# The next group's state update in front of the chunk's output work, in each step of a chunked scan

## The chip, the cores and the metric

One Trainium2 chip, one of its cores. The metric is device time in microseconds of one execution of the whole program, median of the runs of a kernel. The core has a matrix engine (TensorE: PE for matmuls, PEld for its weight loads), VectorE (DVE), ScalarE (ACT), GpSimd (POOL) and SyncE (SP), which here issues all the DMAs. Each engine works through its own instructions strictly in the order in which they stand in the program, and waits at an instruction until what that one needs is there.

## The reference, cut to what matters

The program is one layer of a network over 1024 latent tokens and 256 context tokens of width 1024. The part that the change touches is a bidirectional state-space scan: 8 groups of 4 heads, chunks of 128 tokens (8 latent chunks and 2 context chunks), and for each direction

```
states   = einsum('bcsgn,bcsgj,bcsgjp->bcgjpn', bc, decay_to_end, xdt)     # per chunk
carry    = carry * chunk_decay + states                                     # from chunk to chunk
cb       = einsum('bclgn,bcsgn->bcgls', cc, bc)
y_diag   = einsum('bcgjls,bcsgjp->bclgjp', cb * lmat, xdt)                  # inside a chunk
y_off    = einsum('bclgn,bcgjpn,bclgj->bclgjp', cc, entering, exp(a_cum))   # from the carried state
```

The carry runs over the chunks forwards in one direction and backwards in the other, so the output of a group's first chunk needs the last state of the backward direction: all states of a group have to stand before its outputs begin. After the scan come a gate, a grouped norm, a Fourier branch, projections, and a gated feed-forward block.

## The kernel before

The stage of the scan walks over 64 ticks, 8 groups of 8 chunks (the loop at L1016). While the outputs of group g are worked out, the states of group g+1 are built, one per tick and two in a group's last tick (9 per group: context and latent chunks). So that PE is never without work, large matmuls of other parts, the projections by which the later stages are fed, are laid between: `run_fill`, whose matmuls are called `fill` in all rows (L203, L204, L205 and L210).

The kernel is written in a layer that records every operation and then orders each engine's instructions by itself, with a timing model of its own; the order in which the operations are written sets who goes first where several could go. The pieces of a tick, by function:

- `state_a(i)` (L869): the chunk's inputs times the decay weights, the forward half on DVE (tile `xwf`, L873), the backward half on POOL (`xwb`, L874). Both tiles have two buffers.
- `state_b(i)` (L877): two matmuls into the PSUM tile `st` (L881, L882), which has one buffer, and then eight DVE operations of 64 columns (L891) that make the new states, `S0` forwards and `S1` backwards, from the state before and `st`. For a group's first state two ACT copies (L887) stand in their place. The next `st` matmul waits until these have read `st`.
- `y_load(c)` (L896): the DMAs of the next chunk, `abc` among them (L900: a row of 1024 numbers spread over the 128 partitions; two buffers).
- `y_a(c)` (L904): matmuls `cb` (L908) and `yo` (L910, L911; L911 reads the backward states `S1`), one PSUM buffer each; eight ACT operations on `abc` (L915), a masked copy on DVE (L917), an exponential on ACT (L918); on DVE the product `G` (L920), `cd` and `dg` (L924, L925) and `y2` (L929); on POOL `xd` (L932, then two additions, L934 and L935).
- `y_b`, `y_b2` (L938, L946), one tick later: the matmuls `yd` (L943, one PSUM buffer) from `G`, then on DVE `yz` (L951, which frees `yd` and needs `xd` complete; then L952), a norm and a scale.
- `y_c` (L963), four ticks later: transposes (`ytr`, L968) and the store.

The weights of the fill matmuls are split into a high part on ACT (`whi`, L198) and a low part on POOL (`wlo`, L199, 128x1024).

The instructions that the change moves belong to the loop at L1016, in the lines L1027 to L1034.

Of the kernel before, what the change touches and what calls it, by code (L numbers as in the profile page):

```python
# [20 lines left out]
NT = L // P  # L21
# [114 lines left out]
def build(nc, tc, h, o, hook=None, stop=None):  # L136
    es = ExitStack()
    with es:
        _build(nc, tc, h, o, hook, stop, es)


def _build(nc, tc, h, o, hook, stop, es):
# [853 lines left out]
    def run_fill(n):  # L996
        while nfill[0] < n:
            nfill[0] += 1
            try:
                next(fill)  # L1000
            except StopIteration:
                return

    groups = {0: Group(0)}
# [9 lines left out]
    nticks = NG * NT  # L1014
    groups[0].y_load(0)
    for n in range(nticks + LAG + 1):  # L1016
        g, c = divmod(n, NT)
        if n < nticks:
            if c == 0 and g + 1 < NG:
                groups[g + 1] = Group(g + 1)  # L1020
                groups[g + 1].load_states()
                groups[g + 1].state_a(0)
        if n >= 1 and n - 1 < nticks:
            groups[(n - 1) // NT].y_b((n - 1) % NT)
            groups[(n - 1) // NT].y_b2((n - 1) % NT)
        if n < nticks:
            groups[g].y_a(c)  # L1027
            if n + 1 < nticks:
                groups[(n + 1) // NT].y_load((n + 1) % NT)
            if g + 1 < NG:  # L1030
                for i in ((c,) if c < 7 else (7, 8)):
                    if i + 1 < 9:
                        groups[g + 1].state_a(i + 1)
                    groups[g + 1].state_b(i)  # L1034
        if n >= LAG and n - LAG < nticks:
            groups[(n - LAG) // NT].y_c((n - LAG) % NT)
        if n < nticks - NT:
            run_fill(8 + FOFF + ((NPRE - 8 - FOFF) * (n + 1)) // (nticks - NT))
        else:
            run_fill(NPRE + int(RT * (n - 55)))  # L1040
# [668 lines left out]
```

## Time and profile before

| | |
|---|---|
| median of 3 runs | 2228.85 us (2227.23 to 2230.65) |
| profiled execution, its own time | 2232.41 us |
| its span in the trace | 2230.6 us |
| PE busy | 2157.4 us, 97% of the span |
| DVE, ACT, POOL busy | 73%, 45%, 31% |
| stage of the scan | from about 612 us (first fill matmul) to about 1155 us |

The span is what lies between the first and the last instruction in the trace; the time of the same execution is 1.8 us longer. Idle time of an engine that is not the bottleneck costs nothing, so the figure to read in this stage is the idle time of PE, and what ended it.

### The profile page before, as it was taken

The numbers are of one execution on the slowest core, as the hardware profiler recorded it, in microseconds if no ns is written. First come the engines' busy times: TensorE is split into PE (matmuls) and PEld (weight loads), VectorE is DVE, ScalarE is ACT, GpSimd is POOL, SyncE is SP. The second block draws the span as 40 slices with busy tenths as digits, with TensorE's granted clock in tenths as the row PEclk, the third lists the DMA queues.
The fourth block names the chain that finished last, engine by engine and source line by source line (L and its number), as shares of the span: only waits on it lengthen the run. The fifth ranks groups of instructions, "written<-read, shape, count | busy, mean of one in ns | idle before, by whom it ended". The sixth has DMA issues, their size and how long they took to land.

```text
span 2230.6 us, 32729 instructions
## 1 busy us (share of the span) xinstructions
PE 2157.4 (97%) x11560; PEld 1805.8 (81%) x11560; DVE 1628.0 (73%) x2795; ACT 996.0 (45%) x2093; POOL 701.7 (31%) x581
## 2 busy tenths in 40 slices
PE   6999999999999999999999999999899999999997
PEld 1778888887798999999889887877687888878876
DVE  5888888998758777877726657946987667774577
ACT  4444444445436667666743222224532333234443
POOL 1532111010125555555521221111243333332222
PEclk9999999999999999999999999999999999999999
DMA  8212223342454555555454556752476244457765
GB/s 285 77 62 95 76 89 129 126 131 99 149 172 151 175 159 173 175 167 175 151 174 177 178 172 226 246 174 81 155 267 238 86 141 145 144 201 232 235 206 179
DMA packets 167388, 360.80 MB, mean 162 GB/s; under 512 B 17580, under 2 KB 57260, under 8 KB 166584
## 3 DMA queue, kind: packets, MB, share of 16 engines
q1 hardware_dynamic: 167224, 358.71, 47.9%
q8 instruction: 91, 1.49, 0.3%
q14 instruction: 73, 0.60, 0.1%
HBM read 267.86 MB, written 90.78 MB: 161 GB/s over the span
## 4 chain that ended last, share of the span: by engine, by line
PE 74%; DVE 10%; DMA 7%; ACT 4%; issue 3%; POOL 1%; SPq 0%; DVEq 0%; POOLq 0%; ACTq 0%
PE mm L496 16%; PE dm L210 8%; PE fp L204 6%; PE fp L205 6%; PE fp L203 5%; DMA abc<-s_a 3%; PE mm L498 3%; PE spq L210 2%; PE fq L204 2%; PE fq L205 2%; ACT abc L915 2%; PE fq L203 2%; PE fill L210 2%; PE fill L203 2%; PE fill L204 2%
## 5 line engine op out<-in xcount | busy, mean ns | idle before, releaser
L199 POOL TENSOR_TENSOR wlo<-wraw,whi 128x1024 fp32r<-128x1024 f32 x80 | 198.2, 2481 | 581.3 <-ACT whi L198 515.2
L198 ACT CAST whi<-wraw 128x1024 fp32r<-128x1024 f32 x123 | 127.8, 1044 | 218.0 <-PE dm L210 79.3
L203 PE MATMUL fill<-whi,hhi 128*128 128x256 f32 x768 | 222.3, 290 | 0.6 <-ACT whi L198 0.4
L433 DVE SCALAR_TENSOR_TENSOR cv<-pad,vecs,cv 128x1282 f32<-128x1282 f32 (+1 forms) x128 | 211.1, 1679 | 9.4 <-ACT cv L430 8.8
L204 PE MATMUL fill<-wlo,hhi 128*128 128x256 f32 x768 | 216.0, 281 | 0.2 <-POOL wlo L199 0.2
L205 PE MATMUL fill<-whi,hlo 128*128 128x256 f32 x768 | 216.0, 282 | 0.0
L915 ACT ACTIVATE abc<-abc,a_all 128x128 f32<-128x128 f32 x512 | 157.7, 389 | 90.7 <-DMA abc<-s_a 86.7
L205 PE MATMUL fp<-m,opl 128*128 128x512 f32 x452 | 179.7, 398 | 4.3 <-DVE opl L1389 4.1
L203 PE MATMUL fp<-m,oph 128*128 128x512 f32 x452 | 179.7, 398 | 2.1 <-ACT m L1432 0.9
L204 PE MATMUL fp<-m,oph 128*128 128x512 f32 x452 | 179.8, 398 | 1.8 <-DVE m L1433 1.7
L496 PE MATMUL mm<-tq,whi 128*128 128x512 f32 x480 | 155.9, 405 | 2.3 <-ACT whi L198 2.3
L203 PEld LDWEIGHTS fill<-whi,hhi 128*128 128x128 f32 x768 | 144.1, 188 | 3.0 <-ACT whi L198 0.5
L204 PEld LDWEIGHTS fill<-wlo,hhi 128*128 128x128 f32 x768 | 144.6, 188 | 1.4 <-POOL wlo L199 0.6
L205 PEld LDWEIGHTS fill<-whi,hlo 128*128 128x128 f32 x768 | 144.3, 188 | 0.5
L496 PE MATMUL mm<-hhi,whi 128*128 128x512 f32 x320 | 127.5, 399 | 3.4 <-DVE pad L572 3.4
L496 PE MATMUL mm<-hlo,whi 128*128 128x512 f32 x320 | 127.6, 399 | 0.0
L496 PE MATMUL mm<-hhi,wlo 128*128 128x512 f32 x320 | 127.3, 399 | 0.0
L917 DVE COPY_PREDICATED abc<-misc,abc 128x512 f32<-128x512 int32 x64 | 52.0, 813 | 83.4 <-ACT abc L915 83.3
L496 PEld LDWEIGHTS mm<-tq,whi 128*128 128x128 f32 x480 | 91.2, 192 | 24.1 <-ACT whi L198 3.3
L205 PEld LDWEIGHTS fp<-m,opl 128*128 128x128 f32 x452 | 85.2, 189 | 26.5 <-DVE opl L1389 5.6
L891 DVE SCALAR_TENSOR_TENSOR S<-S,ead,st 128x64 f32<-128x64 f32 x512 | 104.8, 272 | 0.0
L203 PEld LDWEIGHTS fp<-m,oph 128*128 128x128 f32 x452 | 85.3, 189 | 24.0 <-ACT m L1432 1.3
(412 smaller groups left out, 5888.7 us busy)
## 6 DMA issues: line engine op xcount, KB each, us to landing
abc<-s_a SPq DMA_DIRECT2D x64, 512.0 KB
fraw<-in_wfi SPq DMA_DIRECT2D x44, 512.0 KB
wraw<-in_wxbc SPq DMA_DIRECT2D x32, 512.0 KB
dx<-in_wada SPq DMA_DIRECT2D x32, 512.0 KB
wraw<-in_wzf SPq DMA_DIRECT2D x24, 512.0 KB
gt<-s_gate SPq DMA_DIRECT2D x24, 512.0 KB
fi<-in_wfo SPq DMA_DIRECT2D x22, 512.0 KB
s_cw<-fo SPq DMA_DIRECT2D x44, 256.0 KB
```

Source lines behind the costliest of these rows:

```text
L198: nc.scalar.copy(out=hi[:, :cols], in_=raw[:, :cols])
L199: (eng or nc.gpsimd).tensor_tensor(out=lo[:, :cols], in0=raw[:, :cols], in1=hi[:, :cols].bitcast(F32), op=ALU.subtract)
L203: nc.tensor.matmul(ps, lhsT=a[0], rhs=b[0], start=start, stop=False)
L204: nc.tensor.matmul(ps, lhsT=a[0], rhs=b[1], start=False, stop=False)
L205: nc.tensor.matmul(ps, lhsT=a[1], rhs=b[0], start=False, stop=stop)
L210: nc.tensor.matmul(ps, lhsT=a[i], rhs=b[j], start=start and (i, j) == (0, 0), stop=stop and (i, j) == (1, 0))
L433: nc.vector.scalar_tensor_tensor(out=v[:, :n], in0=pd[:, t:t + n], scalar=cwh[:, 5 * b + t:5 * b + t + 1], in1=v[:, :n], op0=ALU.mult, op1 ...
L496: nc.tensor.matmul(ps, lhsT=lhs[x], rhs=b[i][y], start=i == 0 and (x, y) == (0, 0), stop=i == 3 and (x, y) == (1, 0))
L498: nc.tensor.matmul(cps, lhsT=lhs[x], rhs=(hc_hi, hc_lo)[y][c0 + i], start=first and i == 0 and (x, y) == (0, 0), stop=last and i == 3 and ...
L891: nc.vector.scalar_tensor_tensor(out=sn[:, hd_], in0=S[-1][:, hd_], scalar=decp[:, i, d, 4 * g + j:4 * g + j + 1], in1=sv_[:, hd_], op0=AL ...
L915: nc.scalar.activation(out=abc[:, d, j, :], in_=abc[:, d, j, :], func=AF.Identity, scale=-1.0, bias=a_all[:, c, hd:hd + 1])
L917: nc.vector.copy_predicated(out=E, mask=tri_b.bitcast(mybir.dt.int32)[:, None, :].to_broadcast([P, HPG, P]), data=abc[:, 1])
```

## The change

In each tick the block that advances the next group's states is written in front of `y_a` and `y_load`, where it stood behind them. No operation is added, removed or altered, and the condition around it is the same.

```diff
         if n < nticks:
-            groups[g].y_a(c)
-            if n + 1 < nticks:
-                groups[(n + 1) // NT].y_load((n + 1) % NT)
             if g + 1 < NG:
                 for i in ((c,) if c < 7 else (7, 8)):
                     if i + 1 < 9:
                         groups[g + 1].state_a(i + 1)
                     groups[g + 1].state_b(i)
+            groups[g].y_a(c)
+            if n + 1 < nticks:
+                groups[(n + 1) // NT].y_load((n + 1) % NT)
         if n >= LAG and n - LAG < nticks:
```

The orders that follow are those that the ordering makes of it. First PE in an ordinary tick of group 1 (rows with - stand before, rows with + now, the others in both; `fill` matmuls stand ahead of the piece and behind it; a number behind a tile's name tells one buffer's use from another):

```order
 L205 MATMUL fill_6540<-whi_6413,hlo7_205 128x256
-L943 MATMUL yd_6568<-xh_5330,G_6470 128x64 x4
-L908 MATMUL cb_6582<-cT_6484,bT_6482 128x128
-L910 MATMUL yo_6584<-S0_5796,cT_6484 128x256
-L911 MATMUL yo_6584<-S1_6146,cT_6484 128x256
-L881 MATMUL st_6615<-xwf_6488,bh_6327 128x256
-L882 MATMUL st_6615<-xwb_6489,bh_6331 128x256
+L881 MATMUL st_6586<-xwf_6455,bh_6327 128x256
+L882 MATMUL st_6586<-xwb_6456,bh_6331 128x256
+L943 MATMUL yd_6568<-xh_5330,G_6487 128x64 x4
+L908 MATMUL cb_6599<-cT_6501,bT_6499 128x128
+L910 MATMUL yo_6601<-S0_5763,cT_6501 128x256
```

The state's two matmuls moved from behind the output matmuls to their front, some 2 us of PE work earlier.

Second DVE where group 4 ends, the tick with two states, before:

```order
L929 TENSOR_TENSOR y2_9884<-yo_9865,ead_212 128x512
L925 SCALAR_TENSOR_TENSOR dg_9881<-dt_all_209,dg_9881,rows_213 128x4
L917 COPY_PREDICATED abc_9894<-misc_171,abc_9894 128x512
L873 TENSOR_TENSOR xwf_10009<-xh_9989,wst_all_211 128x256
L891 SCALAR_TENSOR_TENSOR S0_9903<-S0_9809,ead_212,st_9900 128x64 x4
L891 SCALAR_TENSOR_TENSOR S1_9908<-S1_9814,ead_212,st_9900 128x64 x4
L917 COPY_PREDICATED abc_10054<-misc_171,abc_10054 128x512
L873 TENSOR_TENSOR xwf_10056<-xh_9989,wst_all_211 128x256
L891 SCALAR_TENSOR_TENSOR S0_9916<-S0_9903,ead_212,st_9913 128x64 x4
L891 SCALAR_TENSOR_TENSOR S1_9921<-S1_9908,ead_212,st_9913 128x64 x4
```

And the same states on DVE now:

```order
L929 TENSOR_TENSOR y2_9811<-yo_9792,ead_212 128x512
L925 SCALAR_TENSOR_TENSOR dg_9808<-dt_all_209,dg_9808,rows_213 128x4
L873 TENSOR_TENSOR xwf_10009<-xh_9989,wst_all_211 128x256
L891 SCALAR_TENSOR_TENSOR S0_9870<-S0_9780,ead_212,st_9867 128x64 x4
L891 SCALAR_TENSOR_TENSOR S1_9875<-S1_9785,ead_212,st_9867 128x64 x4
L920 TENSOR_TENSOR G_9908<-abc_9817,cb_9893 128x512
L924 SCALAR_TENSOR_TENSOR cd_9910,dg_9911<-cb_9893,misc_171 128x128
L951 TENSOR_TENSOR yz_9859<-xd_9813,yd_9853 128x256
```

Before, each of the two state updates stood right behind a masked copy (`abc_9894` is that of the next group's first chunk, `abc_10054` that of its second). Now no masked copy stands between `dg` and the first of them, and `G`, `cd` and `yz` stand behind it; the second follows later, behind the masked copy of the next group's first chunk.

Third POOL near the end of group 1, where the low parts of two weight tiles are made, before:

```order
L932 TENSOR_TENSOR xd_6912<-xh_5342,dg_6907 128x256
L934 TENSOR_TENSOR xd_6912<-xd_6912,y2_6910 128x256
L935 TENSOR_TENSOR xd_6912<-xd_6912,y2_6910 128x256
L199 TENSOR_TENSOR wlo_6983<-wraw_6980,whi_6982 128x1024
L199 TENSOR_TENSOR wlo_7643<-wraw_7640,whi_7642 128x1024
```

And now:

```order
L932 TENSOR_TENSOR xd_6929<-xh_5342,dg_6924 128x256
L199 TENSOR_TENSOR wlo_6983<-wraw_6980,whi_6982 128x1024
L934 TENSOR_TENSOR xd_6929<-xd_6929,y2_6927 128x256
L199 TENSOR_TENSOR wlo_7643<-wraw_7640,whi_7642 128x1024
L874 TENSOR_TENSOR xwb_7119<-xh_6325,wst_all_211 128x256
L935 TENSOR_TENSOR xd_6929<-xd_6929,y2_6927 128x256
```

The two weight splits stood behind the chunk's three `xd` operations; now they stand between the first of them and the last, with the state's product `xwb`.

## Rows read from the trace of the kernel before

**Rows 1.** The page's first part: engine, busy us, share of the span, instructions.

```profile
PE 2157.4 (97%) x11560; PEld 1805.8 (81%) x11560; DVE 1628.0 (73%) x2795; ACT 996.0 (45%) x2093; POOL 701.7 (31%) x581
```

**Rows 2.** PE's waits, 625 to 1160 us: line, awaited, us in total, times, longest.

```profile
PE st L881 <- DVE S L891: 6.8, 10, 1.7
PE st L881 <- issue: 3.5, 2, 1.9
PE yo L911 <- DVE S L891: 2.9, 2, 1.5
PE cb L908 <- DVE cd L924: 1.1, 1, 1.1
PE yo L910 <- DVE y L929: 0.8, 1, 0.8
PE st L881 <- ACT S L887: 0.7, 1, 0.7
```

**Rows 3.** PE's timeline: start, us, engine, line, operation, idle before and its releaser.

```profile
683.87 0.67 PE L881 MATMUL st<-xwf,bh 128*128 128x256 f32 x2 [1.71 <-DVE S L891]
...
765.87 0.59 PE L881 MATMUL st<-xwf,bh 128*128 128x256 f32 x2
...
812.08 0.67 PE L881 MATMUL st<-xwf,bh 128*128 128x256 f32 x2 [1.86 <-issue]
...
965.08 0.67 PE L881 MATMUL st<-xwf,bh 128*128 128x256 f32 x2 [1.31 <-DVE S L891]
...
1026.02 0.67 PE L881 MATMUL st<-xwf,bh 128*128 128x256 f32 x2 [1.52 <-DVE S L891]
...
1032.71 0.70 PE L911 MATMUL yo<-S,cT 128*128 128x256 f32 x2 [1.48 <-DVE S L891]
```

**Rows 4.** PE's timeline, for the pace of each kind of matmul.

```profile
660.21 0.28 PE L204 MATMUL fill<-wlo,hhi 128*128 128x256 f32 x1
660.32 0.59 PE L881 MATMUL st<-xwf,bh 128*128 128x256 f32 x2
660.75 0.59 PE L882 MATMUL st<-xwb,bh 128*128 128x256 f32 x2
...
687.61 1.00 PE L943 MATMUL yd<-xh,G 128*128 128x64 f32 x8
688.45 0.44 PE L908 MATMUL cb<-cT,bT 128*128 128x128 f32 x2
688.72 0.60 PE L910 MATMUL yo<-S,cT 128*128 128x256 f32 x2
```

**Rows 5.** DVE's timeline in a tick with two weight splits on POOL.

```profile
804.44 2.13 DVE L952 TENSOR_TENSOR yz<-yz,zs 128x256 f32<-128x256 f32 x1
...
810.36 1.61 DVE L891 SCALAR_TENSOR_TENSOR S<-S,ead,st 128x64 f32<-128x64 f32 x8
```

**Rows 6.** POOL's timeline in the same tick: a weight split, an addition.

```profile
803.89 2.39 POOL L199 TENSOR_TENSOR wlo<-wraw,whi 128x1024 fp32r<-128x1024 f32 x1
...
811.67 0.73 POOL L935 TENSOR_TENSOR xd<-xd,y 128x256 f32<-128x256 f32 x1
```

**Rows 7.** POOL again, near the end of group 1.

```profile
764.36 2.36 POOL L199 TENSOR_TENSOR wlo<-wraw,whi 128x1024 fp32r<-128x1024 f32 x1 [0.37 <-ACT whi L198]
767.92 2.41 POOL L199 TENSOR_TENSOR wlo<-wraw,whi 128x1024 fp32r<-128x1024 f32 x1 [1.20 <-ACT whi L198]
```

**Rows 8.** DVE's timeline where group 4 ends.

```profile
961.79 0.76 DVE L917 COPY_PREDICATED abc<-misc,abc 128x512 f32<-128x512 int32 x1 [1.56 <-ACT abc L915]
...
963.33 1.61 DVE L891 SCALAR_TENSOR_TENSOR S<-S,ead,st 128x64 f32<-128x64 f32 x8
```

**Rows 9.** ACT's timeline where the loop over the groups starts.

```profile
670.53 2.44 ACT L915 ACTIVATE abc<-abc,a_all 128x128 f32<-128x128 f32 x8 [4.28 <-DMA abc<-s_a]
672.88 0.62 ACT L887 COPY S<-st 128x256 f32<-128x256 f32 x2
```

**Rows 10.** One line's instructions: duration in ns, least, median, longest.

```profile
L952 DVE TENSOR_TENSOR yz<-yz,zs x64: 401/421/2527, 674.3 to 1137.8; 128x256 f32<-128x256 f32 x64
```

## The prediction

> **What bounds the kernel now.** I read the page's first part first: PE is busy 97% of the span [rows 1], so time can only come from PE's idle stretches or go into new ones; the change adds no work to any engine. Then the list of PE's waits in the stage of the scan [rows 2]. It adds up to 6.8 + 3.5 + 2.9 + 1.1 + 0.8 + 0.7 = 15.8 us. That is the most the change can give back, 0.7% of the kernel. Most of it has one cause: the matmuls `st` and `yo` wait for DVE's state update S (6.8 and 2.9). The 3.5 put down to "issue" are two waits of `st` in which the profile names no releaser. For one of them the timeline of DVE does: S starts at 810.36, takes 1.61, ends at 811.97, and `st` starts at 812.08 [rows 3, 5]. So these are waits for S too.
>
> PE's timeline [rows 3] tells where the waits lie, and I sort them in four heaps.
> - Start of the loop over the groups, up to 684 us: 1.1 (`cb`), 0.8 (`yo` for `y2`), 0.7 (`st` for the ACT copies), 1.71 (`st` for S), and of the 2.9 of `yo` what is not at 1032.71, 1.4. Sum 5.7.
> - Group ends, where two states fall in one tick: 1.31, 1.52, 1.48, and three small ones. The ten waits of 6.8 are 1.71, 1.31, 1.52 and seven more that share 2.3, so a small one is 0.33, three are 1.0. Sum 5.3.
> - The two ticks with a pair of weight splits on POOL: 3.5.
> - Four small ones elsewhere: 2.3 less 1.0, 1.3.
>
> Why S is late at a group end is seen on DVE: the masked copy waits for ACT, starts at 961.79, and only then S at 963.33 to 964.94; `st` follows at 965.08 [rows 3, 8]. Before, S stood in DVE's queue behind the masked copy of the next group, which waits for a DMA and ACT.
>
> **The change, part by part.** Prices on PE [rows 4]: a fill matmul 0.11, a pair `st` or `yo` twice 0.43, so 0.87, `yd` 0.84, `cb` 0.27 (I take 0.27 for `ytr` too).
>
> Group ends, now: the first of the two S stands ahead of `G`, with no masked copy in front. The second stands behind one, that of the next group's first chunk, the very one that ran at 961.79 to 962.55. If it runs then again, that S ends at 964.94 as before. PE asks for it later than before: it came to its `st` at 965.08 - 1.31 = 963.77, and in the new order it has by then one more `st`, one more `yd` and four fill matmuls behind it, 0.87 + 0.84 + 0.44 = 2.15, so it comes at 965.9, with 1.0 to spare. `yo` at 1032.71 is covered in the same way, since the next group's first `st`, which needs the same S, stands ahead of it. The heap of 5.3 goes.
>
> Ticks with split pairs: on DVE the product `yz` took 2.13 while a split ran on POOL from 803.89 to 806.28; its median is 0.42 [rows 5, 6, 10]. S stood behind it and five more operations. Now S of that tick stands ahead of `G`, `cd` and `yz`; between two `st` PE has 0.27 + 0.87 + 0.27 + 24 fills of 0.115, 4.2 in all, and S with the product before it needs 1.61 + 0.4. One loss of 1.7 still fits. The heap of 3.5 goes.
>
> The Trainium skill, page "SBUF — State Buffer", section "Who interferes with whom", says that DVE and GpSimd share a port pair by an exclusive lock, which a DVE operation with two SBUF inputs needs against a GpSimd operation that reads SBUF. The long `yz` agrees with that; S, with one input in PSUM, would be free of it. If instead a split struck any DVE operation alike, the sum above would be the same, as one loss fits.
>
> Start: PE came to the `st` that waits for the ACT copies 0.7 early, and they ended at 673.50 [rows 9]. Now that `st` stands one `yo` (0.87) and that one's wait (0.8) earlier, while the copies move up by one of eight `abc` operations, 0.3. That wait grows by 0.87 + 0.8 - 0.3 = 1.4. The 1.71 behind it may shrink, since S stands further forward there too. Bounds -0.3 and +1.4; I take +0.7, halfway.
>
> What is pushed back: `G`, `cd`, `y2` and `dg` come behind S, about 2 us later on DVE, and on POOL the state's product and the weight splits come in between `xd`'s operations. In eight ticks with a state a split now stands between the first and the last of them; before, in one. `yz` waits for the last, and the next `yd` waits for `yz`. Near the end of group 1: if the splits run when they ran, 764.36 to 766.72 and 767.92 to 770.33 [rows 7], then `xwb` and the last addition at 0.73 each [rows 6] end at 771.8, `yz` at 772.2. PE's `cb` of that tick came 0.27 + 0.87 ahead of 765.87 [rows 3], at 764.73; from there to `yd` the order has `cb`, `yo`, `ytr`, 35 fills, `st`, `cb`, `yo`, `ytr`: 0.27 + 0.87 + 0.27 + 4.0 + 0.87 + 0.27 + 0.87 + 0.27 = 7.7, 772.4. That is 0.2 to spare, in three of the eight ticks. In the five others one split or a longer way leaves about 1.0. The splits themselves wait for ACT by 0.37 and 1.20 [rows 7], so a shift of up to 1.2 is in the rows: a tick costs 0 to 1.0. I take 0.5 for the three and 0.2 for the five, 2.5.
>
> The DMA of `abc` for two chunks on is issued when `G` has freed its buffer, so it starts up to 2 us later. No wait of PE names it, and nothing of S at the first state of a group end hangs on it now; I cost it at nothing, and its price, if that cover is gone, is in the second rival.
>
> Sum: -5.3 - 3.5 + 0.7 + 2.5 = -5.6. The profiled execution would take 2232.41 - 5.6 = 2226.8. It lies 3.6 above the median of the runs; on the median the forecast is 2228.85 - 5.6 = 2223.3. Its own range: at best both heaps and the 1.3 go, and the start gives 0.3: -10.4, 2218.5; at worst +1.4 at the start and eight times 1.0: +0.6, 2229.5.
>
> **The rivals.**
> 1. Slower: POOL becomes what PE waits for. In the eight ticks the last `xd` addition stands behind splits that come later than before by a split's whole length, 2.4; less the spare 0.5 that is their mean, PE waits 1.9 eight times, 15.2. Sum -8.8 + 0.7 + 15.2 = +7.1: 2236.0. It decides from 1.0 per tick (8.1 / 8). For it: the spare of 0.2. Against it: PE's waits name POOL nowhere of weight now, and ACT makes `whi` as PE frees the buffers, in the same place as before.
> 2. The change doesn't do what it says: the masked copy comes as late as `G` moves, up to 2 us, so the second S of a group end is as late against its `st` as before. The 5.3 stay: -3.5 + 0.7 + 2.5 = -0.3, 2228.5. For it: 4.28 of idle time on ACT ahead of `abc` for its DMA [rows 9]. Against it: the spare of 1.0.
> 3. Both splits of a pair strike the products that now stand right ahead of S, `xwf` and `yz`: S is 3.4 late, 2.2 fit, PE waits 1.2 once in each of six groups, 7.2. Sum -5.6 + 7.2 = +1.6, 2230.4. The page's lock would make this possible, since both products have two SBUF inputs; the rows show the loss for `yz` alone.
>
> **How the numbers follow.** Chances: forecast 0.62, rival 1 0.14, rival 2 0.17, rival 3 0.07. What a measurement tells from no change is 0.2%, 4.5 us. Two thirds of the forecast's range lie beyond a gain of 4.5, which is 0.42, and a little of rival 2 adds to that: faster 0.44. The rest of the forecast and rivals 2 and 3 are the same: 0.41. Slower 0.15: rival 1 and a rest. The range: from 2218.5, the forecast's best end, to 2231.0, which takes in rivals 2 and 3 and leaves out most of rival 1.
>
> **What would show it.** In the profile after, PE's waits in this stage should add up to about 10 us instead of 15.8. `st` for S should be short at group ends, and no `yo` should wait for S past the start. The wait for the ACT copies at the start should be near 2. New rows should name `yd` waiting for DVE's `yz`, about 0.3 each. Wrong would be: `yd` waiting over 1 us in several ticks (rival 1), waits of `st` for S of over 1 us at group ends (rival 2), or S late behind long `xwf` and `yz` (rival 3). If PE's waits fall as said and the time doesn't, the loss lies past the scan.

## The result, and the profile after

The changed kernel takes 2258.74 us (median of 4 runs, 2257.63 to 2261.06), the kernel before 2229.75 us beside it (2227.23 to 2234.23): a ratio of 1.0126, 95% interval 1.0107 to 1.0145. It is 29 us slower, where 5.6 us faster was forecast, and lies far outside the range. The profiled execution took 2261.06 us, its span is 2259.3.

First the page's first part, after (compare [rows 1]):

```profile
PE 2174.1 (96%) x11560; PEld 1819.9 (81%) x11560; DVE 1632.7 (72%) x2795; ACT 999.7 (44%) x2093; POOL 704.8 (31%) x581
```

PE runs the same 11560 matmuls, but is busy 16.7 us longer with them. So there are two losses: PE waits more, and PE is slower. Nearly all of the time lies in the stage of the scan. The first matmul `sab` of the next stage (L1103) starts at 1194.30 instead of 1165.02, 29.3 later (the stage itself begins 1.7 later), and the span is 28.7 longer. Windows over the stage, from its first `fill` to the first `sab`, tell the two apart: length, busy time of PE, PEld, DVE, ACT and POOL with instruction counts, granted clock of TensorE, share of the DMA engines, GB/s. First the kernel before, then after, with five short windows of after:

```profile
612.24:1165.02 552.78, 535.46 (x3857) 500.42 (x3856) 383.43 (x1196) 346.09 (x1048) 276.63 (x323) 1.00 0.51 166
```

```profile
613.94:1194.30 580.36, 548.76 (x3857) 511.47 (x3855) 393.91 (x1197) 349.81 (x1048) 277.94 (x323) 0.98 0.50 158
730.00:740.00 10.00, 9.65 (x63) 9.40 (x64) 6.94 (x21) 5.14 (x18) 5.76 (x7) 0.83 0.70 224
760.00:770.00 10.00, 7.83 (x47) 7.17 (x47) 8.27 (x31) 5.13 (x16) 3.28 (x5) 0.83 0.29 79
860.00:870.00 10.00, 7.63 (x46) 7.12 (x46) 7.07 (x18) 5.73 (x20) 7.80 (x8) 0.83 0.63 202
990.00:1000.00 10.00, 8.08 (x49) 7.57 (x50) 6.98 (x18) 5.58 (x20) 7.33 (x8) 0.83 0.56 202
1070.00:1080.00 10.00, 4.64 (x25) 4.08 (x24) 5.97 (x16) 7.72 (x21) 2.89 (x2) 0.83 0.32 110
```

The same 3857 matmuls. PE's idle time is 552.78 - 535.46 = 17.3 before and 580.36 - 548.76 = 31.6 after: 14.3 more waiting. Its busy time is 548.76 - 535.46 = 13.3 more: that is the clock for the most part. The granted clock of before is 1.00 over the stage; after, it falls to 0.83 in the five windows shown, and to 0.96 and 0.53 between 660 and 680. Windows of 1 us (the missing share of the clock times PE's busy time) put what this loses at about 12 us, an estimate, some 4 of them between 669 and 680. So over the stage the loss is nearly twice the added waits.

PE's waits between 625 and 1190, after (total us, times, longest):

```profile
PE ytr L968 <- ACT yst L971: 12.8, 7, 5.4
PE yd L943 <- DVE G L920: 6.3, 3, 2.4
PE yo L910 <- DVE y L929: 3.3, 4, 1.2
PE fill L203 <- ACT whi L198: 2.2, 3, 0.9
PE cb L908 <- DVE cd L924: 1.5, 1, 1.5
PE st L881 <- issue: 1.4, 1, 1.4
PE st L881 <- DVE S L891: 1.0, 2, 0.5
PE fill L203 <- DVE zs L803: 0.9, 1, 0.9
PE fill L210 <- ACT gt L821: 0.5, 1, 0.5
PE fill L203 <- ACT ust L807: 0.5, 2, 0.2
```

Against [rows 2]: `st` for S fell from 6.8 to 1.0, `yo` for S is gone, as forecast. But the list adds up to 30.4 instead of 15.8 (16.4 with two waits of `fill` that [rows 2] leaves out), and its two first rows are new: the transposes `ytr` wait for the copies `yst` on ACT that free their one PSUM buffer (12.8), and `yd` waits for `G` (6.3).

The three waits for `G` have one pattern, on DVE and POOL, after. The first in full, with the masked copy ahead of it, and the product `yz` of the two others:

```profile
725.79 0.74 DVE L917 COPY_PREDICATED abc<-misc,abc 128x512 f32<-128x512 int32 x1 [3.39 <-ACT abc L915]
727.09 2.60 DVE L952 TENSOR_TENSOR yz<-yz,zs 128x256 f32<-128x256 f32 x1
729.62 0.67 DVE L920 TENSOR_TENSOR G<-abc,cb 128x512 f32<-128x512 f32 x1
...
859.14 2.59 DVE L952 TENSOR_TENSOR yz<-yz,zs 128x256 f32<-128x256 f32 x1
988.66 2.61 DVE L952 TENSOR_TENSOR yz<-yz,zs 128x256 f32<-128x256 f32 x1
...
726.77 2.64 POOL L199 TENSOR_TENSOR wlo<-wraw,whi 128x1024 fp32r<-128x1024 f32 x1 [4.74 <-ACT whi L198]
```

Right ahead of each late `G` stands a `yz` of 2.6 us where the median is 0.42, while a weight split runs on POOL (from 726.77, 858.80 and 988.34). The excess, 2.2, is about the length of the waits (1.76, 2.37, 2.19). The masked copy ahead of it had waited 3.1 to 3.4 for ACT's `abc`, and the split 4.7 to 5.2 for `whi`, which stands behind the same activations on ACT. So a late landing and a slow product come together here.

The timeline of one of the waits of `ytr`, after, where group 4 ends (start, duration, engine, line, tiles, count, and in brackets the idle time before it and what ended it):

```profile
937.93 0.38 PE L968 MATMUL ytr<-misc,yz 128*128 128x128 f32 x2
943.74 0.44 PE L968 MATMUL ytr<-misc,yz 128*128 128x128 f32 x2 [2.63 <-ACT yst L971]
...
934.71 0.40 SPq L900 DMA_DIRECT2D abc<-s_a  x1
...
939.30 2.45 ACT L915 ACTIVATE abc<-abc,a_all 128x128 f32<-128x128 f32 x8 [3.61 <-DMA abc<-s_a]
941.66 0.36 ACT L802 ACTIVATE zs<-fill 128x256 f32<-128x256 f32 x1
941.92 0.40 ACT L953 ACTIVATE xd<-yz 128x256 f32<-128x256 f32 x1
942.23 0.19 ACT L953 ACTIVATION_READ_ACCUMULATOR xd<-yz 128x1 f32 x1
942.55 0.63 ACT L918 ACTIVATE abc<-abc 128x512 f32<-128x512 f32 x1
943.08 0.61 ACT L971 ACTIVATE yst<-ytr,vecs 128x128 f32<-128x128 f32 x2
```

The transposes of one chunk were ready to be copied at 938.3. ACT stood idle then, at the head of its queue the first activation of another chunk's `abc`, whose transfer had been issued at 934.71 and landed at 939.30. The eight activations, three small operations and the exponential stood ahead of the copies, which ended at 943.69. PE came to the next transposes at 943.74 - 2.63 = 941.11, only 3.2 after the first. The kernel before also waits on ACT for `abc` (86.7 us in all in this stretch, 114.4 after), but no `ytr` waits there; what PE pays for it there goes by way of the masked copy and S (the runs without the transfer, below). PE's order differs too. The start of a chunk's transposes, less the idle time in front of it, less the start of the chunk's before, is under 4.3 us once before (from 690 to 1165) and 13 times after, from 710.79 to 1102.90; all seven `ytr` waits are behind intervals of 3.2 to 3.8.

### The profile page after: what moved, and what is told of

Read it like the earlier page. It is cut to its first block, busy times and chain, and to the rows that moved or that the text cites. A ratio compares the mean times of both kernels' runs of the same rounds, so it can differ in the third digit from the quotient of the medians.

```text
span 2259.3 us, 32715 instructions
## 1 busy us (share of the span) xinstructions
PE 2174.1 (96%) x11560; PEld 1819.9 (81%) x11560; DVE 1632.7 (72%) x2795; ACT 999.7 (44%) x2093; POOL 704.8 (31%) x581
## 4 chain that ended last, share of the span: by engine, by line
PE 69%; DVE 14%; DMA 7%; ACT 4%; issue 3%; POOL 2%; SPq 0%; DVEq 0%; POOLq 0%; ACTq 0%
PE mm L496 15%; PE dm L210 6%; PE fp L204 6%; PE fp L205 6%; PE fp L203 6%; DMA abc<-s_a 4%; PE mm L498 3%; PE fq L204 2%; PE fq L205 2%; PE fq L203 2%; PE spq L210 2%; PE fill L210 2%; ACT abc L915 2%; PE fill L203 2%; PE fill L204 2%
## 5 line engine op out<-in xcount | busy, mean ns | idle before, releaser
L915 ACT ACTIVATE abc<-abc,a_all 128x128 f32<-128x128 f32 x512 | 159.3, 390 | 117.3 <-DMA abc<-s_a 114.4
```

The lines of the kernel that those rows point to most:

```text
L915: nc.scalar.activation(out=abc[:, d, j, :], in_=abc[:, d, j, :], func=AF.Identity, scale=-1.0, bias=a_all[:, c, hd:hd + 1])
```

## The experiments

Each was timed in alternation with the kernel before; ratios are to that, with 95% intervals.

**Which part of the move, and is it the buffer of `abc`?** Four kernels. The first gives `abc` a third buffer (`name="abc", bufs=2` becomes 3).

> The changed kernel with a third abc buffer. On DVE 83 of the 64-column state operations stand between a masked copy and its G (81 in the changed kernel, 28 in the one before), so the order is kept and only the tie between G and the abc transfer two chunks on is cut. Theory A (the ring: G frees abc, the transfer lands some 4.7 us later, ACT waits for it, and the ytr copies that PE needs stand behind it on ACT): PE's waits in the scan fall from 30 to about 10 us, ytr for yst under 3 us, no granted clock under 1.00 past the start, time 2222 to 2232. Rival B (S ahead of G is bad by itself, since yd waits for G and yo for y2): the waits stay near 30 us, time 2252 to 2262. Rival C (the loss comes from the two states of a group's last step): as B.

The second and third put the state block in front in a group's last step alone, and in the other seven alone:

```diff
-            if g + 1 < NG:
+            if g + 1 < NG and c == 7:      # third kernel: c < 7; the other steps' block stays behind y_load
```

> The state block stands in front of y_a only in a group's last step (two states), behind it in the seven others. On DVE 26 state operations stand between a masked copy and its G. Theory A (the ring, made longer by S ahead of G): time as before, 2225 to 2233. Rival B (S ahead of G): the same. Rival C (the two states of a group's last step): most of the loss is here, 2245 to 2260.

> The state block stands in front of y_a in the first seven steps of a group, behind it in the last one (two states). On DVE 77 state operations stand between a masked copy and its G. Theory A and rival B: the loss stays, 2248 to 2262, with ytr and yd among PE's waits and the granted clock falling several times. Rival C: time as before, 2225 to 2235.

The fourth cuts `y_a` in two:

```diff
+            groups[g].y_a(c)          # cb, yo, abc, G
             if g + 1 < NG:
...
-            groups[g].y_a(c)
+            groups[g].y_a2(c)         # cd, dg, y2, xd
```

> The changed kernel with y_a cut in two behind G: first cb, yo, the abc operations and G, then the state block, then cd, dg, y2 and xd. On DVE 29 state operations stand between a masked copy and its G. Theory A: G frees abc as early as before, time 2224 to 2234, idle time of ACT for abc near 87 us instead of 114. Rival B (S also late for nothing, but y2 and xd behind S): if it is y2, cd and xd that hurt rather than G, the loss stays, 2245 to 2260, with yo for y2 and yz for xd among the waits.

Measured: third buffer 2252.87 (1.0101, 1.0081 to 1.0122); last step alone 2230.63 (1.0000, 0.9984 to 1.0016); the seven others alone 2253.71 (1.0107, 1.0088 to 1.0126); `G` in front 2229.16 (0.9996, 0.9982 to 1.0010). So rival C falls: the loss is in the seven ordinary steps. Theory A in its first form falls too (it had 2222 to 2232 for the third buffer): the waits stay, as these rows of ACT's and PE's waits in that kernel show:

```profile
ACT abc L915 <- DMA abc<-s_a: 102.5, 54, 5.3
PE ytr L968 <- ACT yst L971: 13.9, 6, 5.0
PE yd L943 <- DVE G L920: 7.0, 3, 2.7
```

ACT still stands in front of the landing 54 times. That left B and a second form of A, which I call D: what matters is what stands behind `abc` on ACT.

**Is it the copies behind `abc` on ACT, or S ahead of `G`?** Four more. In the first two the first half of `abc` goes to a tile of its own, so that the masked copy reads `abc` last:

```diff
+            E = pb.tile([P, HPG, P], F32, name="E", bufs=2)
...
-                    nc.scalar.activation(out=abc[:, d, j, :], in_=abc[:, d, j, :], ...
+                    nc.scalar.activation(out=(E if d == 0 else abc[:, 1])[:, j, :], in_=abc[:, d, j, :], ...
-            E = abc[:, 0]
```

> The changed kernel, in which the four activations of the first half of abc write a tile E of their own (two buffers), so that abc is read for the last time by the masked copy and its next transfer no longer waits for G. On DVE 109 state operations stand between a masked copy and its G, more than the 81 of the changed kernel. Theory D (a late G issues the abc transfer late, ACT stands still in front of abc, and what stands behind that on ACT, the ytr copies above all, is what PE waits for; a third buffer did not help because ACT's order used it to come to abc earlier): idle time of ACT for abc under 50 us, ytr for yst under 3 us, time 2222 to 2235. Rival B (S ahead of G is bad by itself, through yd for G and yo for y2): time 2248 to 2262, with yd for G at 6 us or more.

> The kernel before with the same tile E. On DVE 30 state operations stand between a masked copy and its G. Theory D: ACT's idle time for abc falls as well, but no wait of PE hung on it, so 2220 to 2232. Rival B: the same. What it tells: whether E itself costs or gains anything, and so what the run of the changed kernel with E is to be read against.

In the third the two lines of `y_c` stand ahead of the state block in the loop.

> The changed kernel with y_c (ytr and its two copies on ACT) written ahead of the state block. On DVE 85 state operations stand between a masked copy and its G. Theory D: if the ordering puts the copies ahead of abc on ACT, the ytr waits (12.8 us) go and with them the clock falls behind them, 2235 to 2246; the waits of yd for G (6.3 us) stay. Rival B: the ytr waits matter little, 2250 to 2262.

In the fourth the copies go to DVE:

```diff
-                nc.scalar.activation(out=self.yst[:, hh, c % 2, :], in_=tp[:, hh * P:hh * P + P], func=AF.Copy,
-                                     scale=vecs[:, gi:gi + 1])
+                nc.vector.tensor_scalar(out=self.yst[:, hh, c % 2, :], in0=tp[:, hh * P:hh * P + P], scalar1=vecs[:, gi:gi + 1],
+                                        scalar2=1.0, op0=ALU.mult, op1=ALU.mult)
```

> The changed kernel with the two copies of ytr on DVE instead of ACT (0.6 us more on DVE per chunk). On DVE 87 state operations stand between a masked copy and its G. Theory D: the ytr waits are no longer behind ACT's wait for abc; DVE waits for the same abc at its masked copy, so part of them comes back there: ytr under 6 us, time 2235 to 2252. Rival B: yd for G stays or grows with the longer DVE, 2250 to 2265.

Measured: with E 2265.56 (1.0165, 1.0144 to 1.0186), the kernel before with E 2235.08 (1.0031, 1.0017 to 1.0044), `y_c` first 2250.64 (1.0101, 1.0078 to 1.0124), copies on DVE 2240.81 (1.0057, 1.0037 to 1.0076). The run with E missed D's forecast, lies above B's range too, and its rows show how:

```profile
ACT abc L916 <- DMA abc<-s_a: 131.3, 50, 5.1
PE ytr L968 <- ACT yst L971: 10.3, 10, 1.9
```

The transfer was freed earlier, and ACT's wait for it grew, from 114.4 to 131.3: the activations of `abc` had moved forward in ACT's order with it. The kernel before with E missed its forecast as well (2220 to 2232): seven `ytr` wait 6.0 us for `yst` in it, though only one interval between its transposes is under 4.3 us. So such a wait doesn't need close transposes. With the copies off ACT, over half of the loss came back (1.0126 to 1.0057): `ytr` waits 4.9 in all, `yd` for `G` 0.2, and the granted clock stays at 1.00 past the start. `y_c` first took away most of the `ytr` waits (3.2), and only one interval between transposes is under 4.3 there; but `st` for S came back (7.3), `yd` for `G` stays (4.7), PE's idle time is still 27.1 in the stage, and the time lies in B's range. B was not dead yet: 87 state operations stand ahead of `G` on DVE with the copies moved, and 13.7 us were still missing to the kernel before (2240.81 against 2227.16).

**The transfer left out, and what the moves themselves cost.** Theory F, below, is D with the spacing of the transposes added. For the first two the transfer of each chunk goes (the load of the first row and the scale of the exponential are left out of the diff):

```diff
-            abc = pb.tile([P, 2, HPG, P], F32, name="abc", bufs=2)
-            nc.sync.dma_start(out=abc.rearrange("p a b c -> p (a b c)"), in_=s_a[self.g, c]...
...
+            abc = pb.tile([P, 2, HPG, P], F32, name="abc", bufs=2)
...
-                    nc.scalar.activation(out=abc[:, d, j, :], in_=abc[:, d, j, :], ...
+                    nc.scalar.activation(out=abc[:, d, j, :], in_=abr0[:, d, j, :], ...
```

> The changed kernel without the abc transfer of each chunk (left out: all chunks read the row of the first one, and the exponential has scale 0, so its values are 1; every instruction of ACT and DVE stays). On DVE 62 state operations stand between a masked copy and its G. Theory F (PE's order puts the transposes of two chunks 3.2 to 4.1 us apart, 13 times instead of once, and ACT needs longer between their copies since it stands waiting for the abc transfer, which lands 4 to 5 us after its issue): without the transfer ACT's wait is gone, ytr for yst under 3 us, the clock does not fall past the start, time 2222 to 2238. Rival B (S ahead of G, through yd and yo): time 2245 to 2260.

> The kernel before with the same transfers left out, as the yardstick for the run of the changed kernel. Theory F: no wait of PE hung on abc, so 2220 to 2231. Rival B: the same. If it falls by as much as the changed kernel does, the transfer costs both alike and tells nothing of the change.

The third writes only `cb` and `yo` ahead of the state block, the fourth moves the copies to DVE in the kernel before.

> The changed kernel in which only the four matmuls of cb and yo are written ahead of the state block; the activations of abc, the masked copy, G and all the rest stand behind it. On DVE 29 state operations stand between a masked copy and its G, transposes on PE keep the spacing of the kernel before. Theory F (all hangs on the state's matmuls standing ahead of cb and yo on PE): time as before, 2224 to 2235. Rival H (it is the activations of abc and G, written behind the state, that make the loss): 2248 to 2262.

> The kernel before with the two copies of ytr on DVE. Theory F: no wait of PE hung on these copies here, so no gain, 2225 to 2234, and what the changed kernel with the same edit lacks to the kernel before (13 us) belongs to the state's place. Rival I (the move itself costs, by a longer DVE): 2236 to 2245, and then the 13 us are the price of the move.

Measured: without the transfer 2219.09 (0.9963, 0.9950 to 0.9976) after the change and 2216.13 (0.9953, 0.9936 to 0.9969) without it; `cb` and `yo` first 2229.96 (1.0010, 0.9998 to 1.0022); the kernel before with copies on DVE 2236.46 (1.0041, 1.0026 to 1.0056). PE's longest waits of the changed kernel without the transfer, up to 1165:

```profile
PE st L881 <- DVE S L891: 4.8, 5, 1.5
PE st L881 <- issue: 1.4, 1, 1.4
...
```

No `ytr`, no `yd` for `G`, though 12 intervals between transposes are still under 4.3 us and 62 state operations still stand ahead of `G`. By the transfer's absence the changed kernel falls from 1.0126 to 0.9963, the one before from 1 to 0.9953, and their intervals overlap: the loss is gone, and B falls with it. Both came out below their forecasts (2222 to 2238 and 2220 to 2231). For the kernel before that was a miss in kind: the forecast said that no wait of PE hung on `abc` there, but it gains 11.9 us, and `st` for S, 6.8 in [rows 2], is gone from its waits. The same landing costs both kernels, then, and the changed one some 26 us more. The move of the copies to DVE costs 0.4% by itself, against F's forecast of 2225 to 2234, so the 13.7 us that were missing are mostly its own price: with the copies on DVE the two orders stand at 1.0057 and 1.0041, with intervals that overlap. And with `cb` and `yo` written ahead of the state nothing is lost. That run doesn't tell PE's order from DVE's: with the four matmuls DVE's order went back too (29 state operations between a masked copy and its `G`, 28 in the kernel before, 81 in the changed one).

**The transfer left in, but in time.** One thing was still argued: that a landing in time would do what leaving the transfer out does. The first pair gives E a single buffer (`name="E", bufs=1`).

> The changed kernel with the tile E for the first half of abc, as before, but with one buffer of E instead of two: now the activations of abc can't start before the previous chunk's G has read E, while the transfer is issued at the masked copy two chunks back. On DVE 98 state operations stand between a masked copy and its G. If a third buffer and the earlier release did not help because ACT's order used them to come to abc as early as before, in front of the transfer's landing, then here ACT comes later, its idle time for the abc transfer falls under 40 us, ytr for yst under 4 us, and the time is 2222 to 2240. If a late G costs by itself, the chain from G to G is now longer, and the time is 2255 to 2280.

> The kernel before with the tile E of one buffer. On DVE 31 state operations stand between a masked copy and its G. If ACT's wait for the abc transfer goes and nothing else comes, 2216 to 2230, and it is a candidate that beats both kernels; if the chain from G over E to the next G becomes what PE waits for (yd for G), 2232 to 2250.

Measured: 2264.01 (1.0159, 1.0135 to 1.0183) and 2239.97 (1.0043, 1.0026 to 1.0060). Both lie in the ranges for a late `G` that costs by itself, but `yd` waits no longer for it than in the changed kernel (6.3), and in the kernel before with this E not at all; `ytr` waits 12.5 and 5.4. The pair did not do what it was made for: only the half of the activations that writes E was held back, the other half went in front, and ACT's wait for the transfer was 144.0. The second pair lets all eight write a tile with one buffer:

```diff
-            abc = pb.tile([P, 2, HPG, P], F32, name="abc", bufs=2)
-            nc.sync.dma_start(out=abc.rearrange("p a b c -> p (a b c)"),
+            abr = pb.tile([P, 2, HPG, P], F32, name="abr", bufs=2)
+            nc.sync.dma_start(out=abr.rearrange("p a b c -> p (a b c)"),
...
-            g, abc = self.g, self.abc
+            g, abr = self.g, self.abr
+            abc = pb.tile([P, 2, HPG, P], F32, name="abc", bufs=1)
...
-                    nc.scalar.activation(out=abc[:, d, j, :], in_=abc[:, d, j, :], ...
+                    nc.scalar.activation(out=abc[:, d, j, :], in_=abr[:, d, j, :], ...
```

> The changed kernel in which all eight activations of abc write a tile of their own with one buffer (the transfer fills a raw tile with two buffers). They can't start before the previous chunk's G has read that tile, and the raw tile is free as soon as the activations have read it, so the transfer is issued more than a chunk ahead. On DVE 65 state operations stand between a masked copy and its G. If ACT's wait in front of the landing is what the loss hangs on: ACT's idle time for the transfer under 30 us, ytr for yst under 4 us, no granted clock under 1.00 past the start, time 2220 to 2238. If a late G costs by itself: the chain from one G to the next is one chunk long now, yd for G over 8 us, 2250 to 2280.

> The kernel before with the same raw tile and single buffer. On DVE 28 state operations stand between a masked copy and its G. With the transfer out of ACT's way 2216 to 2230, and then it may beat both kernels; if the chain from G to G binds, yd for G among the waits and 2232 to 2250.

Measured: 2216.19 (0.9955, 0.9938 to 0.9971) with the change and 2217.05 (0.9958, 0.9943 to 0.9974) without it. Both beat both kernels, and the change makes no difference any more. The first lies below its range, and its granted clock fell once past the start (0.83 from 1140 to 1150), which the forecast excluded. All waits of PE between 625 and 1190 in the changed kernel with this edit, and ACT's for the transfer in the whole trace:

```profile
PE sab L1104 <- DMA U<-s_u: 1.9, 1, 1.9
PE st L881 <- DVE S L891: 1.6, 2, 1.2
PE st L881 <- issue: 1.4, 1, 1.4
PE yo L911 <- DVE y L930: 1.0, 2, 0.5
PE st L881 <- PE yo L912: 0.9, 1, 0.9
PE st L881 <- ACT S L887: 0.3, 1, 0.3
PE sc L1087 <- ACT bt L1122: 0.3, 1, 0.3
PE cb L909 <- DVE cd L925: 0.2, 1, 0.2
...
ACT abc L916 <- DMA abr<-s_a: 3.7, 1, 3.7
```

7.6 us in all, and ACT waits for the transfer once instead of 55 times. Of the intervals between transposes 11 are under 4.3 us, nearly as many as in the changed kernel, and no transpose waits. Two chunks of it, 3.3 us apart on PE, with ACT between them:

```profile
982.41 0.38 PE L969 MATMUL ytr<-misc,yz 128*128 128x128 f32 x2
985.67 0.27 PE L969 MATMUL ytr<-misc,yz 128*128 128x128 f32 x1
...
982.83 0.62 ACT L972 ACTIVATE yst<-ytr,vecs 128x128 f32<-128x128 f32 x2 [0.38 <-PE ytr L969]
984.02 2.45 ACT L916 ACTIVATE abc<-abr,a_all 128x128 f32<-128x128 f32 x8 [0.56 <-DVE G L921]
```

The activations of `abc` now wait for `G`, and the copies stand in front of them.

## Why the prediction was wrong

- **The heap of the group ends** (5.3): right. `st` for S is 1.0 in two waits of at most 0.5, and no `yo` waits for S.
- **The heap of the ticks with split pairs** (3.5): the two waits put down to "issue" are gone, but a loss of their kind came back elsewhere. Before, a `yz` made slow by a split stood ahead of S; now three such products stand ahead of `G`, and `yd` waits 6.3 for it. The forecast asked whether S could bear a slow product, and not whether `G` could.
- **Start** (+0.7): the wait for the ACT copies, 0.7 before and near 2 by forecast, is gone: they end at 674.75, and the `st` behind them starts at 675.58 without a wait. The row of 1.4 put down to "issue" (at 670.03) is, by DVE's timeline, a wait for S, which ends there at 669.93. The waits of the start add up to 3.7 instead of 5.7. Not foreseen was the granted clock of 0.53 between 670 and 680, which costs more than that gain (about 4, the estimate above).
- **What is pushed back, on POOL** (2.5, and rival 1): it did not come. No row names `yd` waiting for `yz`. In rival 1 the mean spare of three ticks at 0.2 and five at 1.0 is 0.7 and not 0.5, so its sum should have been 13.6 and not 15.2.
- **"The DMA of `abc` ... I cost it at nothing"**: this step failed. I looked for who waits for `G` and for S, and the price "if that cover is gone" was that of a late S alone, 5.3. I did not ask what stands behind `abc` on ACT. There stand the copies that free the transposes' PSUM buffer, and `whi`, on which the splits wait. With the transfer's late landing ahead of them `ytr` waits 12.8, and `yd` 6.3 for a `G` that a late masked copy and a slow `yz` hold up together. That the loss hangs on the landing is shown: with it out of ACT's way the two orders can't be told apart, whether the transfer is left out (2219.09 and 2216.13 us) or in time (2216.19 and 2217.05). That the copies on ACT belong to it is borne out by the two orders with the copies on DVE (1.0057 and 1.0041). Why the new order pays some 26 us more for the same landing is argued only: PE comes back to the transposes' buffer 3.2 to 4.1 us later 13 times instead of once, and all seven `ytr` waits are there; but with `y_c` first that spacing is gone and most of the loss stays. The idle 4.28 of ACT for `abc` stood in [rows 9]; I used it for a rival about the masked copy only.
- **A term that was missing**: TensorE's clock. Of the 27.6 us by which the stage grew, 14.3 are waits and 13.3 are longer busy time, most of it matmuls at the lower clock. No term had it, since the clock of before is 1.00 throughout the stage, with waits of up to 1.86 [rows 3].
- **Rival 2** foresaw a late masked copy, but as a gain that fails to come. Rival 1 did not happen. Rival 3 had a split striking a product, but ahead of S; it struck ahead of `G`. None of the three had the copies on ACT, so the chance of 0.15 for slower was attached to the wrong mechanism.

Why the ordering packs the transposes when the state's matmuls come first stays open; that it does is in the traces. How much of the 6.3 is the landing's and how much the slow product's is not told apart either: in the changed kernel with the raw tile a `yz` of 2.60 leaves no wait. That the activations of `abc` are moved forward whenever a buffer lets them fits three kernels (131.3 and 144.0 us of waiting, and still 102.5 with a third buffer), and is not shown to be its rule.

The Trainium skill, page "SBUF — State Buffer", section "The DMA setup-cost knee", gives 2 us and the bytes over 436 GB/s for a transfer; for the 512 KB of `abc` that makes an estimate of 3.2 us. From the issue at 934.71 to ACT's start at 939.30 it took 4.6, so the trace lies above it, in a stage where the DMA engines are half busy (0.50 in the window).

## What to carry to other kernels

When an edit delays a buffer's release, follow the transfer into the engine that reads it first, and ask what stands behind that reader in its queue: here a copy that frees a PSUM buffer. A third buffer gave little here (2252.87 against 2258.74), as the reader still came before the landing; reading the transfer into a raw tile and working in a single-buffered tile took the wait away, in the kernel before too. And look for what a new wait of PE does to its clock: in the six kernels here whose stage grew by over 15 us, the stage grew by 1.4 to 2.0 times the added idle time of PE.

## What was not expected of the hardware

PE is busy 95% of the stage (548.76 of 580.36), and yet past the start its granted clock fell behind single waits of 1.76 to 5.36 us, three of them the waits for `G`. Matmuls of after behind the wait of 1.76 for `G` at 730.35, and after the clock was back:

```profile
730.35 1.34 PE L943 MATMUL yd<-xh,G 128*128 128x64 f32 x6 [1.76 <-DVE G L920]
...
732.45 0.41 PE L205 MATMUL fill<-whi,hlo 128*128 128x256 f32 x1
732.66 0.41 PE L203 MATMUL fill<-whi,hhi 128*128 128x256 f32 x1
...
736.73 0.28 PE L204 MATMUL fill<-wlo,hhi 128*128 128x256 f32 x1
736.85 0.28 PE L205 MATMUL fill<-whi,hlo 128*128 128x256 f32 x1
```

The pitch of the same matmul is 0.21 first and 0.12 then: the two levels, 1.2 and 2.4 GHz. It is not the length of the wait alone that decides: the wait of 2.63 at 943.74 left the clock at 1.00. The Trainium skill, page "TensorE: Matmul & The Clock Gate", section "HAM oscillation — how this bites in real kernels", tells of matmuls that start at the lower clock behind a wait for a transfer. The trace agrees in that, with about 12 us lost here by the estimate above; but PE's waits here are for ACT and DVE, which stand behind the transfer, and four of the five are of 1.76 to 2.37 us, shorter than those of the page's example.
